# A conformer and Mamba-2 layer on one core: half of the input projection in block products of seven instead of eight

## The chip, the cores and the metric

The kernel runs on one core of one Trainium2 chip. Its time is the device time of one execution in microseconds, and lower is better. Of each kernel the median of several runs is compared; one more execution was profiled. TensorE (PE) does the matrix products, into PSUM; VectorE (DVE) and ScalarE (ACT) do elementwise work and read PSUM; GpSimd (POOL) does next to nothing here; SyncE (SP) issues the DMA transfers.

## The reference, cut to what matters

The layer takes 1024 prompt tokens and 32 sample tokens of 1024 channels. All branches come out of one projection with 11,296 columns:

```
proj = x @ w_in + b_in
a_val, a_glu, a_gate, z, xbc, dt_raw, g_a, g_b, g_p = split(proj)

u = a_val * sigmoid(a_glu)
u = causal_dwconv(u, buf_a, conv_a_w, conv_a_b)                  # width 31
u = silu(layer_norm(u, norm_a_g, norm_a_b)) * silu(a_gate)
out_a = u @ w_a_out

xbc = silu(causal_dwconv(xbc, buf_b, conv_b_w, conv_b_b))         # width 4
xs, B, C = split(xbc)
dt = softplus(dt_raw + dt_bias);  A = -exp(a_log)
y, h_new = ssd_scan(xs, dt, A, B, C, h0)                          # 4 groups of 8 heads, state 128
out_b = gated_rmsnorm(y + d_skip * xs, z, gnorm_w) @ w_b_out

merged = sigmoid(g_a) * out_a + sigmoid(g_b) * out_b
ple = sigmoid(g_p) * (p @ w_ple)
y = layer_norm(alpha * x + merged @ w_out + ple, ln_g, ln_b)
```

Outputs are y, the last rows of both convolutions, and the state of the scan, for prompt and sample. All of it is float32.

## The kernel before

Channels lie on the 128 partitions and tokens on the free axis: 1056 columns, which are the prompt's 1024 and the sample's 32. A large product is a float32 product of three passes. Both operands are split exactly into a rounded part hi and a rest lo (`split`, `w_split`: ACT writes hi, DVE subtracts and writes lo), and `three` (L266) sums hi*lo, lo*hi and hi*hi in PSUM.

The program is a list of slots with equal PE time. A slot (`slot`, L279) multiplies one tile of weights, 1024 x 128, with x: 8 row tiles k, three passes, three column groups of 352, so 72 matmuls. The PSUM banks of the groups rotate over 0, 1, 2. ACT evicts each group, with the bias. The slots run in this order:

- Slot 1, with the 48 matmuls of dt mixed in, as the rows of x arrive (L405 on). dt goes through softplus and sums in the steps `dt1` to `dt10`, laid over the following slots.
- The input projection in 88 slots, by SSM group: a pair of conv-a tiles (glu, val), B, C and four xs tiles of the group, eight gate tiles that are written out to DRAM, another conv-a pair, four z tiles. Two slots of the embedding product p W_ple (`ple`) stand ahead of group 1.
- 16 slots of out_b, 8 of out_a and the merge, and 32 short slots of w_out with the closing LayerNorm, in four quarters of the tokens (268, 268, 264 and 256 columns).

The SSD scan of a group starts two slots behind its last xs tile and runs in nine chunks, one chunk a slot (`ssd_group`): transposes, the product of C and B, the masked decays, the products with the state, and the product S of XS and B that updates the state. S is made in three passes, with XS and B split.

What stands on DVE in a slot is set by hand: `at(slot, stage, function)` puts a step into a stage of a slot, and what is left of the slot is filled from a queue, `run_fill`, up to a limit of estimated DVE time (8000 to 12300 ns). The queue holds the taps of the 31-wide convolution (conv a, L156, 1086 columns each). The 4-wide convolution (conv b) is three taps of 1059 columns for each B, C or xs tile. Weights are loaded two slots ahead and split one slot ahead. All loads and stores go through SP in program order.

SBUF tiles for activations come out of pools of 32 pieces of 1064 columns (T) and five of 1116 (U).

Of the kernel before, what the change touches and what calls it, by code (L numbers as in the profile page):

```python
# [43 lines left out]
WA, WB = NT + LA, NT + LB    # columns that a conv computes  # L44
# [4 lines left out]
G_GATE, G_GA, G_GB = 0, 16, 24        # first gate tile of a kind  # L49


def slot_tiles():
    """(kind, index, first column in w_in) of the slots of the first half."""
    pair = lambda t: [("glu", t, O_GLU + 128 * t), ("val", t, O_VAL + 128 * t)] if t < 8 else []
    out = pair(0)
    for g in range(4):
        if g == 1:
            out += [("ple", 0, None), ("ple", 1, None)]
        out += [("B", g, O_B + 128 * g), ("C", g, O_C + 128 * g)]
        out += [("xs", 4 * g + j, O_X + 128 * (4 * g + j)) for j in range(4)]  # L60
# [29 lines left out]
class Units:  # L90
    """Fixed pieces of SBUF (or PSUM) handed out in program order."""
# [24 lines left out]
def emit(nc, tc, I, O, ctx):  # L116
    cpool = ctx.enter_context(tc.tile_pool(name="const", bufs=1))
    wpool = ctx.enter_context(tc.tile_pool(name="w", bufs=2))
    tpool = ctx.enter_context(tc.tile_pool(name="t", bufs=1))
    dpool = ctx.enter_context(tc.tile_pool(name="scr", bufs=1, space=bass.MemoryType.DRAM))  # L120
    ppool = ctx.enter_context(tc.tile_pool(name="ps", bufs=1, space=bass.MemoryType.PSUM))

    spool = tc.tile_pool(name="ssd", bufs=1)
    sp = spool.__enter__()

    T = Units(tpool, 32, 1064, "t")
    U = Units(tpool, 5, 1116, "u")
# [22 lines left out]
    def tt(out, a, b, op):  # L150
        dve[0] += 75 + 1.04 * width(out)
        nc.vector.tensor_tensor(out, a, b, op)  # L152

    def stt(out, a, s, b, op0, op1):
        dve[0] += 135 + 1.04 * width(out)
        nc.vector.scalar_tensor_tensor(out, a, s, b, op0, op1)  # L156

    def tsc(out, a, s1, s2, op0, op1=None):
        dve[0] += 75 + 0.6 * width(out)
        if op1 is None:  # L160
            nc.vector.tensor_scalar(out, a, s1, None, op0)
        else:
            nc.vector.tensor_scalar(out, a, s1, s2, op0, op1)
# [7 lines left out]
    def mm(out, l, r, start=True, stop=True):  # L171
        nc.tensor.matmul(out, l, r, start=start, stop=stop)  # L172

    # the weights of dt: for each row tile 32 columns of hi, 32 of lo, and 64 that are not looked at
    wdt = T.get([P, 1024], F32R, "wdt")
    wd3 = wdt[:, :].rearrange("p (k c) -> p k c", k=8)
    nc.gpsimd.memset(wd3[:, :, 64:].bitcast(F32), 0.0)

# [38 lines left out]
    todo = defaultdict(list)  # L217
    busy = set()                 # slots that also run SSD products
# [40 lines left out]
    def split(raw, name):  # L259
        hi = tget((P, NT), F32R, name + "h")  # L260
        lo = tget((P, NT), F32R, name + "l")
        act(hi, raw)
        tt(lo, raw, hi[:, :].bitcast(F32), ALU.subtract)
        return hi, lo

    def three(ps, wh, wl, xh, xl, first, last):  # L266
        mm(ps, wh, xl, first, False)
        mm(ps, wl, xh, False, False)
        mm(ps, wh, xh, False, last)
# [9 lines left out]
    def slot(s, nm, nk, rhs, evac):  # L279
        """The products of one slot: nm output tiles with nk operand tiles each."""  # L280
# [39 lines left out]
        run_fill(8000.0 if s < 10 else (11400.0 if s < 25 else 12300.0) if ("pe", s) in busy else 10000.0)  # L320
# [4 lines left out]
    def bcast_pe(src, bks):  # L325
        """Sum over the partitions, on all partitions."""
# [30 lines left out]
        # both parts of V are exact, and so are their products with one  # L357
# [51 lines left out]
    w1raw = wpool.tile([P, 1024], F32, tag="wraw", name="wraw1", bufs=2)
    xraw = []  # L410
    for k in range(8):
        t = tget(name="xraw")
        for c0, c1 in GR if k == 0 else ((0, NT),):
            load(t[:, c0:c1], I["xT"][k * P:(k + 1) * P, c0:c1])
        xraw.append(t)
        if k < 2:
            sl = slice(0, 256) if k == 0 else slice(256, 1024)
            load(w1raw[:, sl], I["w_src"][1][:, sl])
        if k == 3:
            load(par, I["par"])  # L420
# [783 lines left out]
    for x in xT:  # L1204
        tput(*x)
# [213 lines left out]
```

## Time and profile before

| | us |
|---|---|
| median of three runs | 1578.08 |
| lowest and highest of them | 1575.24, 1578.16 |
| span of the profiled execution | 1573.9 |
| PE busy in it | 1559.6 (99%) |
| DVE busy | 1151.5 (73%) |
| ACT busy | 723.6 (46%) |
| mean DMA rate | 128 GB/s |
| mean granted clock of PE | 0.997 |

The profiled execution's own time is its span, from the first to the last instruction. Busy times are the sums of the instructions of an engine, without overlaps; PEld is the loading of weights into the array, which runs beside the products. The ends of matmuls are modelled, so how long one matmul takes in a row of them is read from start to start. The chain that ended last is the sequence of work followed back from the last instruction, each step to what released it. In a line of a timeline the first number is the start, the second the duration.

### The profile page before, as it was taken

Reading aid. Unit: us, or ns where it says so; the run is one execution under the profiler, and the core shown is the slowest. Engines: PE = TensorE matmul, PEld = TensorE weight load, DVE = VectorE, ACT = ScalarE, POOL = GpSimd, SP = SyncE. Lnnn points to the kernel's source line nnn. Section 1 sums busy time; section 2 is a strip of 40 time slices with the busy share of each in tenths; the row PEclk is TensorE's granted clock in tenths of the full one; section 3 lists DMA queues with packets and bytes.
Section 4 is the critical chain, followed back from the end, with each engine's and each line's share of the span. In section 5 each row is a group of like instructions: output and inputs, shape, how many; then the busy total and the mean of one; then the engine's idle time right before and its main releaser. Section 6 shows DMA issues by size and latency. Waiting matters only on the chain.

```text
span 1573.9 us, 25018 instructions
## 1 busy us (share of the span) xinstructions
PE 1559.6 (99%) x10283; PEld 1532.7 (97%) x10283; DVE 1151.5 (73%) x1504; ACT 723.6 (46%) x1257; POOL 3.0 (0%) x14
## 2 busy tenths in 40 slices
PE   8999999999999999999999999999999999999997
PEld 8999999999999999999999999999999999999997
DVE  4769888888448888893988687579877486755554
ACT  5565452354475633346444335554346363423333
POOL 0000000000000000000000000000000000000000
PEclk9999999999999999999999999999999999999999
DMA  5126542234448741144763213466455544323222
GB/s 188 49 61 180 158 135 83 83 121 152 91 96 202 180 147 55 41 137 130 204 200 111 65 52 69 157 193 197 151 206 178 192 141 147 96 96 121 97 84 82
DMA packets 123868, 201.81 MB, mean 128 GB/s; under 512 B 27045, under 2 KB 83109, under 8 KB 123754
## 3 DMA queue, kind: packets, MB, share of 16 engines
q1 hardware_dynamic: 123754, 200.22, 42.6%
q8 instruction: 80, 1.31, 0.4%
q14 instruction: 34, 0.28, 0.1%
HBM read 150.01 MB, written 50.18 MB: 127 GB/s over the span
## 4 chain that ended last, share of the span: by engine, by line
PE 98%; ACT 1%; DVE 1%; issue 0%; DMA 0%; ACTq 0%; SPq 0%; DVEq 0%
PE ps L172 96%; PE ps L703 1%; PE ps L704 0%; DVE dtk_t L544 0%; ACT r_t L166 0%; DVE cb_t L156 0%; ACT dtk_t L166 0%; DMA xraw_t<-in_xT 0%; ACT cbo_t L166 0%; ACT p_t L166 0%; ACT dts_t L166 0%; ACT L166 0%; ACT cb_t L166 0%; ACT vin_t L166 0%; ACT whi L166 0%
## 5 line engine op out<-in xcount | busy, mean ns | idle before, releaser
L152 DVE TENSOR_TENSOR wlo<-wraw,whi 128x1024 fp32r<-128x1024 f32 (+1 forms) x117 | 141.9, 1213 | 162.8 <-ACT whi L166 162.3
L156 DVE SCALAR_TENSOR_TENSOR cae_u<-uin_u,par,cae_u 128x1086 f32<-128x1086 f32 x120 | 161.2, 1344 | 0.0
L166 ACT ACTIVATE whi<-wraw 128x1024 fp32r<-128x1024 f32 (+1 forms) x117 | 122.2, 1045 | 70.7 <-PE ps L172 55.5
L156 DVE SCALAR_TENSOR_TENSOR cao_u<-uin_u,par,cao_u 128x1086 f32<-128x1086 f32 x112 | 150.5, 1344 | 0.0
L156 DVE SCALAR_TENSOR_TENSOR cb_t<-vin_t,par,cb_t 128x1059 f32<-128x1059 f32 x72 | 94.9, 1318 | 17.1 <-ACT cb_t L166 13.6
L166 ACT ACTIVATE vin_t<-ps,par 128x352 f32<-128x352 f32 (+1 forms) x96 | 42.8, 477 | 131.7 <-PE ps L172 131.7
L172 PE MATMUL ps<-x0l_t,whi 128*128 128x352 f32 x264 | 90.1, 341 | 0.2 <-ACT vin_t L166 0.2
L172 PE MATMUL ps<-x0h_t,wlo 128*128 128x352 f32 x264 | 85.9, 325 | 0.0
L172 PE MATMUL ps<-x0h_t,whi 128*128 128x352 f32 x264 | 85.7, 324 | 0.0
L172 PE MATMUL ps<-x2h_t,wlo 128*128 128x352 f32 x264 | 85.4, 323 | 0.0
L172 PE MATMUL ps<-x3h_t,wlo 128*128 128x352 f32 x264 | 85.4, 323 | 0.0
L172 PE MATMUL ps<-x4h_t,wlo 128*128 128x352 f32 x264 | 85.4, 323 | 0.0
L172 PE MATMUL ps<-x3h_t,whi 128*128 128x352 f32 x264 | 85.3, 323 | 0.0
L172 PE MATMUL ps<-x4h_t,whi 128*128 128x352 f32 x264 | 85.3, 323 | 0.0
L172 PE MATMUL ps<-x2h_t,whi 128*128 128x352 f32 x264 | 85.3, 323 | 0.0
L172 PE MATMUL ps<-x1h_t,whi 128*128 128x352 f32 x264 | 85.3, 323 | 0.0
L166 ACT ACTIVATE L_t<-L_t,tk 128x128 f32<-128x128 f32 (+1 forms) x288 | 85.3, 381 | 0.0
L172 PE MATMUL ps<-x2l_t,whi 128*128 128x352 f32 x264 | 85.3, 323 | 0.0
L172 PE MATMUL ps<-x3l_t,whi 128*128 128x352 f32 x264 | 85.3, 323 | 0.0
L172 PE MATMUL ps<-x4l_t,whi 128*128 128x352 f32 x264 | 85.3, 323 | 0.0
L172 PE MATMUL ps<-x5l_t,whi 128*128 128x352 f32 x264 | 85.3, 323 | 0.0
L172 PE MATMUL ps<-x1h_t,wlo 128*128 128x352 f32 x264 | 85.3, 323 | 0.0
(631 smaller groups left out, 4785.2 us busy)
## 6 DMA issues: line engine op xcount, KB each, us to landing
wraw<-in_w SPq DMA_DIRECT2D x87, 512.0 KB, 4.0
L_t<-d_accp SPq DMA_DIRECT2D x32, 512.0 KB, 6.7
d_gate<-gt_t SPq DMA_DIRECT2D x24, 528.0 KB, 5.2
d_yn<-cbo_t SPq DMA_DIRECT2D x16, 528.0 KB, 4.4
yraw_t<-d_yn SPq DMA_DIRECT2D x16, 528.0 KB, 4.7
gs_t<-d_gate SPq DMA_DIRECT2D x16, 528.0 KB, 4.5
cw_t<-in_wo SPq DMA_DIRECT2D x16, 512.0 KB, 5.3
wraw<-in_wb SPq DMA_DIRECT2D x16, 512.0 KB, 3.7
```

What stands on the lines that cost most here:

```text
L152: nc.vector.tensor_tensor(out, a, b, op)
L156: nc.vector.scalar_tensor_tensor(out, a, s, b, op0, op1)
L166: nc.scalar.activation(out, a, f, **kw)
L172: nc.tensor.matmul(out, l, r, start=start, stop=stop)
L703: nc.tensor.transpose(pX[:nt, j * P:(j + 1) * P], XS[j][:, sl], ident)
```

## The change

48 of the 88 projection tiles are taken in 24 pairs. With x cut into two halves of its rows (channels) and two of its columns (tokens), and the two tiles of weights of a pair cut into quarters r11, r12, r21, r22 (the first digit is the tile, the second the half of the rows), the four result blocks are made from seven block products instead of eight. The right operands are fixed for all pairs: B11, D1 = B11 - B12, N2, B21, T3, B22 and T4, with N2 = -(D1 + B22), T3 = B22 - B12 and T4 = -(N2 + B21), formed once at the start (`x_sum`, `x_split`, `t_split`) and kept split. D1 takes the place of B12 in the tiles of x, which is loaded again before the single slots. The left operands are formed for each pair one pair ahead: four sums of quarters and seven splits, 512 columns each (`prep_act`, `prep_dve`).

A block product is 4 row tiles, three passes and two groups of 264 columns: 24 matmuls, 168 a pair. Products 0, 2, 4 and 6 add up in the two banks B0 or B1, by turns, and ACT evicts the running sum after each; products 1 and 5 share the two banks C, and product 3 has A. DVE adds A, product 1 (copied out by ACT) and C to the evicted results.

```
+def pair_tiles():
+    gate = lambda n: ("gate", n, GATE_OFF[n // 8] + 128 * (n % 8))
+    G = lambda n: (gate(n), gate(n + 1))
+    C = lambda t: (("glu", t, O_GLU + 128 * t), ("val", t, O_VAL + 128 * t))
+    X = lambda n: ("xs", n, O_X + 128 * n)
+    return [G(0), G(2), C(0), G(8), G(4), G(10), G(6), C(1), G(12), G(16), G(14), C(2), G(18), G(20), G(22), G(24),
+            C(3), G(26), G(28), G(30), C(4), (("B", 0, O_B), ("C", 0, O_C)), (X(0), X(1)), (X(2), X(3))]
...
+    return ca(5) + bcx(1) + z(0) + ca(6) + bcx(2) + z(1)[:2] + ca(7) + bcx(3) + z(1)[2:] + z(2) + z(3)
...
-    T = Units(tpool, 32, 1064, "t")
-    U = Units(tpool, 5, 1116, "u")
+    T = Units(tpool, 22, 1064, "t")
+    U = Units(tpool, 7, 1116, "u")
...
-        dve[0] += 75 + 1.04 * width(out)
+        dve[0] += 144 + 1.053 * width(out)
...
-        run_fill(8000.0 if s < 10 else (11400.0 if s < 25 else 12300.0) if ("pe", s) in busy else 10000.0)
+        run_fill(14200.0 if ("pe", s) in busy else 11000.0)
...
-                three(S, B2[:nt, :P], B2[:nt, P:], XS2[:nt, :512], XS2[:nt, 512:], True, True)
+                mm(S, B2[:nt, :], M[:nt, :512])
...
+    for m in range(4):
+        for g in range(3):
+            ple_group(m, g)
+            step(2 if m * 3 + g >= 4 else 1)
+    U.put(*praw)
+    step(len(work))
+    for k in range(8):
+        dt_products(k)
+    dt1()
+    pw_hi(0, 0, "r11")
+    pw_lo(0, 0, "r11")
+    x_sum("D1", 0)
+    x_sum("D1", 1)
...
+    def pair_slot(s, oa, ob, ba, bb):
+        for j in range(7):
+            ps = A if j == 3 else C if j in (1, 5) else B
+            wh, wl = pw.pop((i, j))
+            for g in range(2):
+                c = slice(g * HN, g * HN + HN)
+                for k in range(4):
+                    w = slice(k * P, k * P + P)
+                    three(ps[:, g, :HN], wh[:, w], wl[:, w], OPND[j](k, 0)[:, c], OPND[j](k, 1)[:, c],
+                          k == 0 and j in (0, 1, 3), k == 3, j in (2, 4, 5, 6))
...
+            elif j == 6:
+                for p_, d in oa[1]:
+                    tt(d, d, p_(C), ALU.add)
+            prep_act(i, j)
+            prep_dve(i, j)
+            if j == 5:
+                run(s, "d2")
+            run_fill(2820.0 * (j + 1) - 300.0)
...
+    SSD0 = [S_CL + i for i in (1, 10, 21, 31)]
```

Behind the pairs stand 40 single slots as before (conv-a tiles 5 to 7, B, C and xs of groups 1 to 3, all z), and the SSD groups start at the second, 11th, 22nd and 32nd of them. The embedding moves to the very start: its first half, dt, `dt1`, its second half, and only then pair 0. S is one float32 product, with neither operand split. The centring of w_out's columns moves from the projection into out_b and out_a, the variance of branch A's LayerNorm is taken later, in out_b, and pools of pieces are opened as others close.

On PE, a plain slot of before goes from one column group to the next (x5h is the high part of x's row tile 5, whi and wlo the split weights):

```order
L172 MATMUL ps_904<-x7l_t_181,whi_757 128x352
L172 MATMUL ps_904<-x7h_t_180,wlo_759 128x352
L172 MATMUL ps_904<-x7h_t_180,whi_757 128x352
L172 MATMUL ps_930<-x0l_t_135,whi_757 128x352
L172 MATMUL ps_930<-x0h_t_134,wlo_759 128x352
```

In the change, pair 0 goes from product 1 (banks C, here ps_633) to product 2 (banks B, ps_583, into which product 0 went too):

```order
L192 MATMUL ps_633<-x3l_t_111,w_1h 128x264
L192 MATMUL ps_633<-x3h_t_110,w_1l 128x264
L192 MATMUL ps_633<-x3h_t_110,w_1h 128x264
L192 MATMUL ps_583<-n2l_4_517,w_2h 128x264
L192 MATMUL ps_583<-n2h_4_516,w_2l 128x264
```

The matmuls are narrower, the weights change with each product, and product 2 adds to banks that ACT has read in between.

On ACT, the start of before splits w0 (wdt) and then x as it comes:

```order
L166 ACTIVATE wdt_t_74<-w_t_106 128x8x32
L166 ACTIVATE x0h_t_134<-xraw_t_109 128x352 x3
L166 ACTIVATE whi_142<-wraw_108 128x256
L166 ACTIVATE x1h_t_146<-xraw_t_114 128x352 x3
L166 ACTIVATE whi_142<-wraw_108 128x768
```

The change has there, behind the splits of the embedding's operands (pl is the result of the embedding), and later ahead of pair 0's first eviction (ga):

```order
L186 ACTIVATE wq1h<-wq_132 128x512
L186 ACTIVATE pl_u_197<-ps_190 128x352
L186 ACTIVATE wdt<-w_142 128x8x32
L186 ACTIVATE pl_u_197<-ps_201 128x352
L186 ACTIVATE x0h_t_104<-xraw_t_134 128x528
...
L186 ACTIVATE w_4h<-r_0_164 128x512
L186 ACTIVATE t4h_4_568<-xraw_t_134 128x1056
L186 ACTIVATE t4h_4_568<-xraw_t_136 128x1056
L186 ACTIVATE w_5h<-sx_411 128x512
L186 ACTIVATE ga_t_581<-ps_583,par 128x528
```

The split of w0 stands behind an eviction of the embedding, with the splits of x behind it, and the first eviction of pair 0 behind the splits of T4.

On DVE, a B, C or xs tile of before has its conv-b taps between two splits of weights, with nothing of PSUM behind them:

```order
L152 TENSOR_TENSOR wlo_861<-wraw_753,whi_859 128x1024
L163 TENSOR_SCALAR dtk_t_866<-dtk_t_866 128x528
L544 RECIPROCAL dtk_t_866<-dtk_t_866 128x528
L152 TENSOR_TENSOR dtk_t_866<-dtk_t_866 128x528
L152 TENSOR_TENSOR dtk_t_866<-dtk_t_866,dt_t_331 128x264
L156 SCALAR_TENSOR_TENSOR cb_t_876<-vin_t_750,par,cb_t_876 128x1059 x3
L1124 MEMSET vin_t_964 128x3
```

In pair 22 of the change (xs 0 and 1) the taps of the tiles of pair 21 stand ahead of the addition that reads banks C (ps_5893):

```order
L172 TENSOR_TENSOR vin_t_5848<-vin_t_5848 128x232
L172 TENSOR_TENSOR vin_t_5848<-vin_t_5848 128x32
L172 TENSOR_TENSOR w_2l<-sx_5890,w_2h 128x512
L172 TENSOR_TENSOR w_3l<-r_23_5809,w_3h 128x512
L172 TENSOR_TENSOR sx_5890<-r_23_5809,sx_5890 128x512
L176 SCALAR_TENSOR_TENSOR cb_t_5879<-vin_t_5600,par,cb_t_5879 128x1059 x3
L176 SCALAR_TENSOR_TENSOR cb_u_5881<-vin_t_5603,par,cb_u_5881 128x1059 x3
L172 TENSOR_TENSOR vin_t_5845<-vin_t_5845,ps_5893 128x264
L172 TENSOR_TENSOR vin_t_5845<-vin_t_5845,ps_5893 128x232
L172 TENSOR_TENSOR vin_t_5845<-vin_t_5845,ps_5893 128x32
```

Six taps stand between the products' last splits and the addition.

More of the change, by code (lines that the diff above doesn't have):

```diff
@@ L169, in load, with mm @@
         nc.sync.dma_start(dst, src)
[L171 to L177, printed above, removed]
+    def mm(out, l, r, start=True, stop=True, more=False):
+        nc.tensor.matmul(out, l, r, start=start, stop=stop, skip_group_check=more)
     par = cpool.tile([P, NPAR], F32, name="par")
@@ L257, in w_split, with three @@
         wsplit[s] = (hi, lo)
[L259 to L269, printed above, removed]
+    def three(ps, wh, wl, xh, xl, first, last, more=False):
+        mm(ps, wh, xl, first, False, more)
+        mm(ps, wl, xh, False, False, more)
+        mm(ps, wh, xh, False, last, more)
     banks = [0, 1, 2]
@@ L406, in emit @@
     H = 32
-    w0 = tget((P, 8, H), F32, "w0")
-    load(w0, I["wdt"])
[L409 to L420, printed above, removed]
@@ new lines, in emit, with wdt_split @@
+    r_quad(0, 0)
+    r_quad(0, 1)
+    w0 = xpool.tile([P, 8, H], F32, tag="t3l", name="w0", bufs=1)
+    wdt = xpool.tile([P, 1024], F32R, tag="t3h", name="wdt", bufs=1)
+    wd3 = wdt[:, :].rearrange("p (k c) -> p k c", k=8)
+    nc.gpsimd.memset(wd3[:, :, 64:].bitcast(F32), 0.0)
+    load(w0, I["wdt"])
+    r_quad(1, 0)
+    r_quad(1, 1)
+    load(par, I["par"])
+    wq_load(2)
+    wq_load(3)
+    def wdt_split():
+        act(wd3[:, :, :H], w0)
+        tt(wd3[:, :, H:2 * H], w0, wd3[:, :, :H].bitcast(F32), ALU.subtract)
@@ new lines, in ple_group @@
+    def ple_group(m, g):
+        c0, c1 = GR[g]
+        ps = psum(bank())
+        wh, wl = wq[m // 2]
+        for k in range(2):
+            w = slice((m % 2 * 2 + k) * P, (m % 2 * 2 + k) * P + P)
+            three(ps[:, :GN], wh[:, w], wl[:, w], ph[:, k, c0:c1], pl_[:, k, c0:c1], k == 0, k == 1)
+        if g == 0 and m in (4, 6):
+            both = xpool.tile([P, 2, NT], F32, tag=f"t3{'hl'[m // 2 - 2]}", name=f"pl{m}", bufs=1)
+            pls[m], pls[m + 1] = both[:, 0, :], both[:, 1, :]
+        if g == 0 and m < 4:
+            pls[m] = U.get([P, NT], F32, "pl")
+        act(pls[m][:, c0:c1], ps[:, :GN])
+        if g == 2:
+            load(d_ple[m], pls[m])
+            if m < 4:
+                U.put(pls[m])
@@ L587, in emit, with step @@
         at(sl_, stage, fn)
+    work = deque()
+    def step(n):
+        for _ in range(min(n, len(work))):
+            f, *a = work.popleft()
+            f(*a)
+    for n in ("r11", "r21", "r22", "r12"):
+        pw_load(0, n)
+    wq_split(0)
+    for g in range(3):
+        for k in range(2):
+            p_split(k, g)
+    wq_split(1)
+    work.append((wdt_split,))
+    for n in ("B11", "B12", "B21", "B22"):
+        work.extend((x_split, n, k) for k in range(4))
+    work.extend(((wq_split, 2), (wq_split, 3)))
@@ new lines, in emit @@
+    work.extend((x_sum, "N2", q) for q in range(2))
+    work.extend((t_split, "n2", (0, 0), q) for q in range(2))
+    work.extend(((pw_hi, 0, 2, "sx"), (pw_lo, 0, 2, "sx")))
+    work.extend((x_sum, "T3", q) for q in range(2))
+    for m in range(4, 8):
+        for g in range(3):
+            ple_group(m, g)
+            step(1)
+    step(len(work))
+    for n in ("r21", "r22"):
+        pw_load(1, n)
+    pw_hi(0, 3, "r12")
+    pw_lo(0, 3, "r12")
+    for q in range(2):
+        t_split("t3", (0, 1), q)
@@ new lines, in emit, with plain @@
+    x_put((0, 1))
+    x_put((1, 1))
+    pw_sum(0, "sx", "r12", "sx")
+    pw_load(1, "r12")
+    pw_hi(0, 4, "r21")
+    pw_lo(0, 4, "r21")
+    x_sum("T4", 0)
+    x_sum("T4", 1)
+    for q in range(2):
+        t_split("t4", (0, 0), q)
+    x_put((0, 0))
+    x_put((1, 0))
+    pw_hi(0, 5, "sx")
+    new_psum("ps1")
+    def plain(t):
+        return [[(lambda ps, f=lambda u: u: ps[:, :, :HN], t[:, NH * h_:NH * h_ + NH].rearrange("p (g c) -> p g c", g=2))]
+                for h_ in range(2)]
@@ new lines, in emit, with vin_tile, done @@
+    BIAS = lambda i: col(C_BIN + i)
+    def vin_tile(kind, n):
+        vin = tget((P, NT + 2 * LB), F32, "vin")
+        ct = n if kind == "xs" else (16 + n if kind == "B" else 20 + n)
+        nc.vector.memset(vin[:, :LB], 0.0)
+        load(vin[:, LB + TP:2 * LB + TP], I["cache_b"][ct * P:(ct + 1) * P, :])
+        if kind != "xs":
+            BCs[(kind, n)] = []
+        def done(t):
+            if kind == "xs":
+                XSs[n] = t
+            else:
+                BCs[(kind, n)].append(t)
+        return vin, lambda s: conv_b(ct, vin, s, done)
@@ new lines, in half_load, with half_split, b12_load @@
+    def half_load(q):
+        pr["h", q] = raw_tile(("r11", "r21")[q], f"half{q}")
+        load(pr["h", q], I["w_src"][S_CL][:, 512 * q:512 * q + 512])
+    def half_split(q):
+        h_, l_ = split_tile(q, f"half{q}")
+        act(h_, pr["h", q])
+        tt(l_, pr["h", q], h_[:, :].bitcast(F32), ALU.subtract)
+        wsplit.setdefault(S_CL, []).append((h_, l_))
+    def b12_load():
+        raw = xpool.tile([P, 4, NH], F32, tag="n2h", name="b12", bufs=1)
+        for q in range(2):
+            load(raw[:, 2 * q:2 * q + 2, :], I["xT"][2 * q * P:2 * q * P + 2 * P, NH:].rearrange("(k p) c -> p k c", p=P))
+        R[0, 1] = [raw[:, 2 * q:2 * q + 2, :] for q in range(2)]
@@ L1106, in emit, with b12_split @@
+    def b12_split():
+        for k in range(4):
+            x_split("B12", k)
+        R.clear()
+    at(S_CL - 2, "end", half_load, 0)
+    at(S_CL - 2, "end", half_load, 1)
+    at(S_CL - 1, "a1", b12_load)
+    at(S_CL - 1, "d2", b12_split)
+    at(S_CL - 1, "pm", half_split, 0)
+    at(S_CL - 1, "a2", half_split, 1)
+    for i, (ta, tb) in enumerate(PAIRS):
+        s = i + 1
+        cur[0] = s
+        ba, bb = BIAS(2 * i), BIAS(2 * i + 1)
+        (kind, n, _), (kb, nb, _) = ta, tb
         if kind == "glu":
@@ new lines, in emit @@
+        pair_slot(s, oa, ob, ba, bb)
+    guards[0].__exit__(None, None, None)
+    wpool = ctx.enter_context(tc.tile_pool(name="w", bufs=2, reuse_waits="tile"))
+    t2pool = ctx.enter_context(tc.tile_pool(name="t2", bufs=1, reuse_waits="tile"))
+    spool = tc.tile_pool(name="ssd", bufs=1, reuse_waits="tile")
+    sp = spool.__enter__()
+    T.free.extend((t2pool, f"y{i}") for i in range(3))
+    new_psum("ps2")
+    for b in (3, 4, 5, 6, 7, 0, 1, 2):
+        psum(b)
+    banks[:] = [0, 1, 2]
@@ L1197, in emit @@
-        if kind == "ple":
-            slot(s, 4, 2, pT, evac)
-            if n == 1:
-                for x in pT:
-                    tput(*x)
-            continue
-        slot(s, 1, 8, xT, evac)
-    for x in xT:
+                ssd_group(g_, SSD0[g_], Late(4 * g_), BCs[("B", g_)], BCs[("C", g_)])
+        slot(s, 1, 8, X, evac)
+    for x in X:
         tput(*x)
     mg = []
-    banks[:] = [0, 1, 2, 3, 4]
     for s in range(S_OB, S_OA):
+        if s == SSD0[3] + 12:
+            spool.__exit__(None, None, None)
+            x2pool = ctx.enter_context(tc.tile_pool(name="x2", bufs=1, reuse_waits="tile"))
+            T.free.extend((x2pool, f"x{i}") for i in range(2))
+            banks[:] = [0, 1, 2, 3, 4]
```

588 lines of the change are left out of this document (362 added, 226 removed).

## The prediction

> **What bounds the kernel now.** I read the page first: the busy times of the engines and the chain that ended last.
>
> ```profile
> span 1573.9 us, 25018 instructions
> PE 1559.6 (99%) x10283; PEld 1532.7 (97%) x10283; DVE 1151.5 (73%) x1504; ACT 723.6 (46%) x1257; POOL 3.0 (0%) x14
> PE 98%; ACT 1%; DVE 1%; issue 0%; DMA 0%; ACTq 0%; SPq 0%; DVEq 0%
> ```
>
> TensorE (PE) is busy in 99% of the span and carries 98% of the chain. VectorE (DVE) has 422 us free, but over stages that differ. Next, the waits of PE, all there are:
>
> ```profile
> PE ps L172 <- ACT x0h_t L166: 4.3, 1, 4.3
> PE ps L172 <- DVE r_t L152: 2.0, 1, 2.0
> PE ps L172 <- ACT r_t L166: 0.7, 1, 0.7
> PE ps L172 <- ACT vin_t L166: 0.2, 1, 0.2
> ```
>
> Only the 4.3 us to the first product, and 2.7 us near the end, are waits. So time is gained by less matmul work alone, and lost by any wait that the new order brings. Then the windows of a stretch with the SSD scan and of one without it (columns: PE, PEld, DVE, ACT, POOL):
>
> ```profile
> 150.00:240.00 90.00, 90.00 (x634) 86.54 (x633) 75.56 (x118) 41.34 (x91) 0.00 (x0) 1.00 0.54 151
> 253.00:440.00 187.00, 187.00 (x1181) 186.26 (x1181) 138.47 (x142) 81.80 (x132) 0.00 (x0) 1.00 0.39 108
> ```
>
> DVE is busy 84% of the SSD stretch and 74% of the plain one, and PE never stops. Last, the chain, which gives the slots their lengths:
>
> ```profile
> 120.95 11.55 PE ps L172 x72
> ...
> 222.26 0.44 PE ps L703 x4
> 222.70 0.11 PE ps L704
> 222.81 14.57 PE ps L172 x101
> ```
>
> A plain slot is 72 matmuls of 352 columns in 11.55 us, 0.1604 us each. A slot with an SSD chunk is 15.12 us.
>
> **The products.** 48 tiles of the projection leave their 48 slots: 48 x 72 = 3456 matmuls of 352 columns go, 554.4 us at 0.1604. In their place stand 24 x 168 = 4032 of 264 columns. Before has that width in its last stage, w_out, in a stretch where PE had no idle time:
>
> ```profile
> 1525.00 0.28 PE L172 MATMUL ps<-m1l_t,whi 128*128 128x264 f32 x1
> ...
> 1531.93 0.28 PE L172 MATMUL ps<-m4l_t,woh_t 128*128 128x264 f32 x1
> ```
>
> These two stand 57 matmuls apart, so one takes 6.93 / 57 = 0.1216 us: 490.3 us for all, 20.4 us a pair where two slots took 23.1. The term is **-64 us**, from -62 to -66. A matmul's fixed part is small by these rows: 88 columns less are 0.0388 us less, which leaves 0.005 us at no columns.
>
> A rule speaks against this change here. The Trainium skill (TensorE: Matmul & The Clock Gate, section Back-to-back issue gap) gives a sustained spacing of 81 ns at 128 columns and 131 ns at 512, because weight loads count too. An estimate between these two puts 264 columns at 99 ns and 352 at 110, a pair at 16.6 us against 15.9 for two slots, and the term at +17 in place of -64. The rows do not agree: their spacing falls nearly with the columns, so I go by the rows.
>
> **The SSD product S.** The product of XS and B in three passes becomes one float32 product. A chunk of before shows both kinds (the x8 are four float32 products of 128 columns, the x3 are the three passes of 512):
>
> ```profile
> 220.40 1.16 PE L172 MATMUL ps<-cbo_t,hT_t 128*128 128x128 f32 x8
> 221.31 0.95 PE L172 MATMUL ps<-XS,B 128*128 128x512 f32 x3
> 222.10 0.60 PE L703 MATMUL ps<-ident,cbo_t 128*128 128x128 f32 x4
> ```
>
> 512 columns of float32 take 221.31 - 220.40 = 0.91 us, and the three passes 0.79 us from start to start, or 3 x 512 / 352 x 0.1604 = 0.70 by the plain pitch. That is 0.12 to 0.21 us for each of 36 chunks, all on PE: **+6 us**, from +4 to +8. The splits of both operands that go, on ACT and DVE, free those engines in slots where PE never waits for them, and are worth nothing.
>
> **The start.** Before splits x as it lands and computes dt and the first tile with it. After puts half the embedding first, then dt, then the other half, and builds four extra operands (D1, N2, T3, T4) before the third product of pair 0. The bytes that land before w0 are wq0, the embedding input, wq1 and the upper half of x: 0.26 + 1.08 + 0.26 + 2.16 = 3.76 MB. What the queues moved at the start of before:
>
> ```profile
> 0.00:4.00 4.00, 0.00 (x0) 0.00 (x0) 0.42 (x1) 2.02 (x3) 1.94 (x12) 1.00 0.49 141
> 4.00:8.00 4.00, 3.72 (x8) 2.26 (x9) 2.00 (x4) 1.58 (x4) 0.00 (x0) 1.00 0.88 274
> 8.00:12.00 4.00, 4.00 (x17) 3.60 (x17) 2.08 (x4) 2.44 (x6) 0.00 (x0) 1.00 1.03 411
> 12.00:14.00 2.00, 2.00 (x15) 2.00 (x14) 1.60 (x5) 1.93 (x4) 0.00 (x0) 1.00 1.02 417
> ```
>
> The first three windows are 3.30 MB at 12 us; 0.6 MB more (w0 is 0.13) come at 13.4 to 13.7 us. ScalarE (ACT) reaches the split of w0 as its second instruction behind the first embedding splits, and everything behind it waits with it: 16 splits of x of 528 columns, 11 evictions of 352, two weight splits. Their prices, and those of dt, are in ACT's timeline of before:
>
> ```profile
> 12.86 1.09 ACT L166 ACTIVATE x3h_t<-xraw_t 128x1056 fp32r<-128x1056 f32 x1
> ...
> 21.15 1.28 ACT L166 ACT_TABLE_LOAD   x1
> 26.65 1.52 ACT L166 ACTIVATE sg_t<-ps,par 128x352 f32<-128x352 f32 x3 [4.21 <-PE ps L172]
> 28.06 1.05 ACT L166 ACTIVATE whi<-wraw 128x1024 fp32r<-128x1024 f32 x1
> 29.01 0.28 ACT L166 ACTIVATE small<-par 32x1 f32<-32x1 f32 x2
> ...
> 34.08 0.56 ACT L166 ACTIVATE uin_u<-ps,par 128x352 f32<-128x352 f32 x1
> ```
>
> One eviction of 352 is 1.41 / 3 = 0.47 us from start to start; a split of 528 I take as 0.60, a little over half of 1.09. So 0.4 + 16 x 0.60 + 11 x 0.47 + 2 x 0.55 = 16.3 us: ACT is through at 30.0. Then a table load (1.28) and dt1, which took 5.05 us in before (29.01 to 34.06), then the split of the first quarter: DVE can begin the operands at 36.9. Its prices, from its timeline:
>
> ```profile
> 150.70 0.68 DVE L152 TENSOR_TENSOR M<-ps,tk 128x512 f32<-128x512 f32 x1
> 151.30 0.68 DVE L152 TENSOR_TENSOR X<-ps,tk 128x512 f32<-128x512 f32 x1
> ...
> 306.05 1.25 DVE L152 TENSOR_TENSOR cbo_t<-cbo_t,zt_t 128x1056 f32<-128x1056 f32 x1
> 307.21 0.78 DVE L161 TENSOR_SCALAR cao_u<-uin_u,par 128x1086 f32<-128x1086 f32 x1
> ...
> 309.17 1.34 DVE L156 SCALAR_TENSOR_TENSOR cao_u<-uin_u,par,cao_u 128x1086 f32<-128x1086 f32 x1
> 310.43 1.34 DVE L156 SCALAR_TENSOR_TENSOR cae_u<-uin_u,par,cae_u 128x1086 f32<-128x1086 f32 x1
> ```
>
> Start to start, 512 columns are 0.60 us, 1056 are 1.16 and a tap of 1086 is 1.26. From the first quarter's split to the sums of T4, DVE has 9 of 512, 4 of 528 (0.62), 8 of 1056 and 4 with a scalar (1.23): 5.4 + 2.5 + 9.3 + 4.9 = 22.1 us, to 59.0. ACT stands at the split of T4 with the eviction of product 0 behind it; product 2 adds into the same PSUM banks and waits for that eviction. T4's second split (1.0), a quarter's split (0.55) and the eviction (0.62) end at 61.2. By then PE has 228 matmul times of 0.16 to do (144 of the embedding, 48 of dt, 36 worth of 48 narrow ones): 36.6 us. It has lost 24.6 us. Before had done 120 matmuls (19.2 us) when ACT got the first result at 26.6, so it had lost 7.4. PE has nothing from about 53 us, when product 1 is done. What an idle PE costs when it resumes is seen at before's start:
>
> ```profile
> 8.44 0.49 PE L172 MATMUL ps<-x0l_t,whi 128*128 128x352 f32 x1
> 8.73 0.49 PE L172 MATMUL ps<-x0h_t,wlo 128*128 128x352 f32 x1
> ...
> 11.70 0.32 PE L172 MATMUL ps<-x1h_t,wlo 128*128 128x352 f32 x1
> 11.86 0.33 PE L172 MATMUL ps<-x1h_t,whi 128*128 128x352 f32 x1
> ```
>
> The step is 0.29 us, later 0.16; 16 or 17 such slow matmuls are 2.2 us lost. The term is 24.6 + 2.2 - 7.4 = **+19 us**. The low bound is +10 (w0 lands 2 us earlier, dt1 lies half beside other work, no slow matmuls, 2 us of the chain hidden), the high one +25 (instructions cost their durations, 0.08 us more each, and wait for one another).
>
> The Trainium skill (the same page, section What's actually happening) says that the clock of the array is halved after an idle window of about 3.4 us and is back after about as long of work. By it the slow stretch would lose 1.7 us in place of 2.2, and the sum would stand 0.5 lower; the trace of before agrees in the steps of 0.29 us, though not in the granted clock, which its windows above give as 1.00.
>
> **Inside the pairs and behind them.** A pair has on DVE 11 sums and splits of 512 (6.6 us) and three additions out of PSUM (1.9), 8.5 us fixed. The fill lays conv-a taps behind that, about eight (10 us): counted in the order of the instructions, pairs 3 to 21 come to 18.3 to 19.2 us of DVE in 20.4 of PE. That holds, with 1 to 2 us of margin. ACT has seven splits of 512 and four evictions, some 7 us. It breaks in pair 22: six conv-b taps (7.4 us) stand on DVE between the subtraction behind product 4 and the addition that frees banks C, which pair 23 needs 8.8 us after product 4; DVE gets there at about 11.5. That is 3 us. The single slots with SSD chunks have 13.4 us of DVE in 15.1. In out_b the order gives four slots with 14.4, 15.4, 11.9 and 10.7 us in 11.55, because LayerNorm's centring moved there; the last operand of out_a may be 0 to 2 us late. With a late load here and there (0 to 1 us in four pairs) I take **+6 us**, from +1 to +15.
>
> **The sum.** 1573.9 - 64 + 6 + 19 + 6 = 1541 us of span. The median of the runs, 1578.1, stands 4.2 above the profiled span, so the forecast is **1545 us**. The bounds of the terms give 1527 to 1564.
>
> **Rivals.** *The start is free.* If ACT's queue does not hold the splits (w0 early, the embedding's 23 us of products covering the rest), the +19 is gone: 1526. For it: the embedding's products need no x. Against: 3.76 MB stand ahead of w0 and 22 us of DVE behind dt1, both by rows. 0.14.
>
> *DVE sets the pace of the pairs.* At 21.5 us a pair in place of 20.4, 23 x 1.1 = 25 us come on top: 1570. For it: every split waits for its ACT half and three additions wait for PSUM, and the margin is 1 to 2 us. Against: the fill is limited product by product. 0.13, a quarter of it below 1566 and a sixth of it within 0.2% of before.
>
> *DVE's pace beyond break-even, slower.* One mechanism: in a pair, 22 instructions cost their durations, not their starts (+1.8), and stand some 2 us for ACT's halves, so a pair takes 22.5 us: 24 x 2.1 = 50 us, 1595. It is slower than before from 1545 + 33, that is 1.4 us more a pair, 21.8 us. Against: the rows from start to start show the overlap of 0.08 us. 0.07.
>
> *The pitch does not fall with the columns.* At 0.1604 a matmul the pairs cost 647 us, 93 more than before in place of 64 less: 1702. The two rows of 264 columns rule it out, unless products into two banks behave otherwise. The rule of the Trainium skill quoted above points this way (TensorE: Matmul & The Clock Gate, Back-to-back issue gap). 0.01.
>
> *The gain is eaten up.* Several terms at their worse ends together, within 0.2% of before: 0.02.
>
> **How the numbers follow.** The forecast has 0.63. 0.2% is 3.2 us, about what a measurement of this kernel can tell from no change: 1574.9 to 1581.2 is the same. The range takes in the free start and a quarter of the paced pairs, 1523 to 1566; out of it are 0.10 of the paced pairs and 0.10 of the rest. Faster: 0.63 + 0.14 + 0.11 = 0.88; same: 0.02 + 0.02 = 0.04; slower: 0.07 + 0.01 = 0.08.
>
> **What would show it.** Right: 168 matmuls of 264 columns in 20.4 us in the windows of pairs 3 to 21, with no PE wait above 0.5 us; one PE wait of 6 to 9 us near 53 to 61 us, released by ACT's ga; one of about 3 us near pair 23, released by DVE's vin; SSD slots of 15.2 to 15.3 us. Wrong: pairs of over 21 us with waits for DVE's splits (DVE's pace), no wait beyond 3 us before 70 us (the free start), or a pitch of 264 columns above 0.125 us.

## The result, and the profile after

The changed kernel takes **1601.06 us** (median of four runs, 1600.07 to 1601.86), the one before 1577.93 in the same comparison: a ratio of 1.0152, 95% interval 1.0137 to 1.0166. It is slower by 1.5% where 2% faster was forecast. The page of the profile after:

```profile
span 1598.3 us, 26653 instructions
PE 1529.6 (96%) x10823; PEld 1485.9 (93%) x10823; DVE 1295.8 (81%) x1763; ACT 815.5 (51%) x1395; POOL 3.0 (0%) x14
PE 80%; DVE 10%; ACT 4%; issue 2%; DMA 1%; SPq 0%; ACTq 0%; DVEq 0%
```

PE's busy time fell by 30 us, but it no longer carries 98% of the chain: DVE and ACT carry 14%. The waits of PE, the largest five:

```profile
PE ps L192 <- DVE acc_t L172: 20.8, 5, 7.4
PE ps L192 <- ACT ga_t L186: 11.7, 2, 9.9
PE ps L192 <- DVE vin_t L172: 5.3, 1, 5.3
PE ps L192 <- DVE t4l L172: 5.2, 1, 5.2
PE ps L192 <- ACT sg_t L186: 3.8, 1, 3.8
```

The name in a line is what the releaser wrote; the three numbers are the us in total, how often, and the longest. ga_t is the start, and there the forecast holds: product 2 of pair 0 began at 60.73 us, forecast 61.2. t4l is the first product of the program, whose operand bears that name: it began at 5.15 us. vin_t and sg_t are the end of the pairs. The largest, acc_t, are the sums of out_b. One window over out_b, of before and then of after (columns: PE, PEld, DVE, ACT, POOL, granted clock, DMA share, GB/s):

```profile
1187.60:1374.90 187.30, 187.30 (x1167) 187.30 (x1165) 133.96 (x165) 89.30 (x107) 0.00 (x0) 1.00 0.43 147
```

```profile
1172.60:1397.10 224.50, 201.02 (x1199) 196.40 (x1198) 169.86 (x217) 102.71 (x121) 0.00 (x0) 0.95 0.49 175
```

After had reached out_b 15 us sooner than before, and lost 37 there. Its 16 slots are not lengthened evenly. Windows of slots 7, 14 and 15, counted from 0:

```profile
1264.40:1284.10 19.70, 13.57 (x75) 13.28 (x74) 16.70 (x20) 7.81 (x9) 0.00 (x0) 0.86 0.16 54
...
1357.30:1379.20 21.90, 14.54 (x74) 13.99 (x73) 15.56 (x18) 14.95 (x15) 0.00 (x0) 0.77 0.37 125
1379.20:1397.10 17.90, 13.42 (x75) 13.12 (x74) 12.08 (x14) 11.60 (x12) 0.00 (x0) 0.90 0.36 119
```

Three slots of 11.6 us of products took 59.5, which is 24.7 of the 37. In slot 7 DVE has 16.7 us to do (the centring of four LayerNorm tiles and the sums of four more); in slot 14 both DVE and ACT have about 15. What happens in slot 14 stands in ACT's and then DVE's timeline:

```profile
1354.39 1.28 ACT L186 ACT_TABLE_LOAD   x1
1355.68 1.27 ACT L186 ACTIVATE cat_t<-cat_t,par 128x1056 f32<-128x1056 f32 x1
...
1361.13 1.07 ACT L186 ACTIVATE ag_t<-ag_t 128x1056 f32<-128x1056 f32 x1
1362.22 1.28 ACT L186 ACT_TABLE_LOAD   x1
1363.52 2.06 ACT L186 ACTIVATE gs_t<-gs_t 128x1056 f32<-128x1056 f32 x2
```

```profile
1357.92 0.51 DVE L172 TENSOR_TENSOR acc_t<-acc_t,ps 128x352 f32<-128x352 f32 x1
1364.63 1.26 DVE L172 TENSOR_TENSOR acc_t<-acc_t,gs_t 128x1056 f32<-128x1056 f32 x1 [6.20 <-ACT gs_t L186]
1365.81 1.25 DVE L172 TENSOR_TENSOR u0l_t<-cat_t,u0h_t 128x1056 fp32r<-128x1056 f32 x1
1366.98 1.25 DVE L172 TENSOR_TENSOR u1l_t<-cat_t,u1h_t 128x1056 fp32r<-128x1056 f32 x1
1368.15 0.51 DVE L172 TENSOR_TENSOR acc_t<-acc_t,ps 128x352 f32<-128x352 f32 x1
```

ACT works off six silus of branch A and loads a table before it takes the sigmoid of the merge gate. DVE stands 6.20 us for that sigmoid, then does two splits, and only then the addition (1368.15) that frees a PSUM bank. PE, with all banks full, waits.

### The profile page after: what moved, and what is told of

The parts are those of the page before. It is cut to its first block, busy times and chain, and to the rows that moved or that the text cites. A ratio compares the mean times of both kernels' runs of the same rounds, so it can differ in the third digit from the quotient of the medians.

```text
span 1598.3 us, 26653 instructions
## 1 busy us (share of the span) xinstructions
PE 1529.6 (96%) x10823; PEld 1485.9 (93%) x10823; DVE 1295.8 (81%) x1763; ACT 815.5 (51%) x1395; POOL 3.0 (0%) x14
## 4 chain that ended last, share of the span: by engine, by line
PE 80%; DVE 10%; ACT 4%; issue 2%; DMA 1%; SPq 0%; ACTq 0%; DVEq 0%
PE ps L192 78%; DVE cat_t L172 1%; DVE acc_t L172 1%; PE ps L996 1%; ACT L186 1%; DVE yraw_t L176 1%; DVE wlo L172 0%; ACT ag_t L186 0%; DMA d_gate<-ga_t 0%; ACT L_t L186 0%; DVE cb_u L176 0%; DVE cb_t L176 0%; DVE cao_u L176 0%; SPq L189 0%; DVE cae_u L176 0%
## 5 line engine op out<-in xcount | busy, mean ns | idle before, releaser
L172 DVE TENSOR_TENSOR wlo<-wraw,whi 128x1024 fp32r<-128x1024 f32 x65 | 79.3, 1220 | 25.5 <-ACT whi L186 25.1
L186 ACT ACTIVATE whi<-wraw 128x1024 fp32r<-128x1024 f32 x65 | 68.4, 1053 | 22.5 <-PE ps L192 16.5
L192 PE MATMUL ps<-n2l,w_2h 128*128 128x264 f32 x192 | 55.9, 291 | 9.9 <-ACT ga_t L186 9.9
L192 PE MATMUL ps<-t3l,w_4h 128*128 128x264 f32 x192 | 55.5, 289 | 1.7 <-ACT ga_t L186 1.7
L192 PE MATMUL ps<-n2h,w_2h 128*128 128x264 f32 x192 | 55.8, 291 | 0.0
L192 PE MATMUL ps<-n2h,w_2l 128*128 128x264 f32 x192 | 55.4, 288 | 0.0
L192 PE MATMUL ps<-t3h,w_4h 128*128 128x264 f32 x192 | 55.3, 288 | 0.0
L192 PE MATMUL ps<-t3h,w_4l 128*128 128x264 f32 x192 | 55.2, 287 | 0.0
L192 PE MATMUL ps<-t4l,w_6h 128*128 128x264 f32 x192 | 54.8, 285 | 0.0
L192 PE MATMUL ps<-t4h,w_6l 128*128 128x264 f32 x192 | 54.6, 284 | 0.0
L186 ACT ACTIVATE ga_t<-ps,par 128x528 f32<-128x528 f32 x32 | 22.5, 703 | 57.1 <-PE ps L192 57.0
```

What stands on the lines that cost most here:

```text
L186: nc.scalar.activation(out, a, f, **kw)
L192: nc.tensor.matmul(out, l, r, start=start, stop=stop, skip_group_check=more)
```

## The experiments

The theory to test: the time is lost in the order of out_b's work, where bunches on ACT and DVE stand ahead of the additions that free PSUM. The rivals: the amount of DVE work that was moved into out_b (169.86 us against 133.96), and transfers that come late.

**spread** does the same work in another order:

```
-        at(B + 2 + t // 4 * 2, "ld", ca_load, t)
...
-        at(B + 6 + t // 4, "d1", ln_center, t)
...
-        at(B + 12 + t // 3, "a0", u_act, t)
...
+        at(B + t // 4, "ld", ca_load, t)
...
+        at(B + 3 + t // 3, "d1", ln_center, t)
...
+        at(B + 10 + t // 2, "a0", u_act, t)
...
```

> The same work as the change in another order: branch A's LayerNorm is taken two to three slots earlier and three tiles a slot, its scaling and silu two tiles a slot, the sums of w_out's columns and the last quarter's splits in the slots that were light. If the bunches in out_b are the cause (slots 7 and 12 to 15, where DVE and ACT had 16 to 18 us of work in 11.6 of PE), out_b falls from 224.5 us to 190 to 200 and the time by 25 to 34 us, to 1567 to 1576. If the amount of DVE work is the cause (170 us in out_b against 134 before), or the transfers (197 to 256 GB/s there against 147), nothing of it is less here: out_b stays above 216 and the time within 8 us of 1601.

Measured: 1578.31 us, ratio 1.0012 (1.0002 to 1.0021) to before, 23 us less than the change. Out_b as a whole, and slots 14 and 15:

```profile
1174.70:1377.50 202.80, 194.77 (x1199) 190.48 (x1199) 171.88 (x220) 100.27 (x119) 0.00 (x0) 1.00 0.54 195
```

```profile
1353.10:1365.90 12.80, 12.20 (x75) 11.62 (x74) 10.90 (x13) 7.70 (x8) 0.00 (x0) 1.00 0.49 181
1365.90:1377.50 11.60, 11.60 (x74) 11.60 (x74) 10.72 (x15) 5.08 (x5) 0.00 (x0) 1.00 0.68 214
```

DVE's work is no less (171.88 us) and the transfers are faster (195 GB/s), and 22 us are gone. So the order was the cause of that much. The gain is 2 us short of the expected range, and 15 us over before remain in slots 0 to 5.

**no_scale** takes DVE work away without moving anything:

```
+        if k >= 12:
             stt(yraw[k], yraw[k], col(C_GNW + k), rb, ALU.mult, ALU.mult)
```

> Leaves out the scaling of the first 12 operand tiles of out_b by their norms and weights, 12 DVE instructions of 1.24 us, 8 of them in out_b's slots 0 to 7; nothing else is moved. By the bunches only slot 7 gains: 1 to 3 us, 1598 to 1600. By the amount of DVE work, 10 of the 36 us that out_b has more go: about 10 us, 1591. By the transfers nothing: 1601.

Measured: 1588.63 us, 12.4 less. That is nearer to the rival's 10 than to 1 to 3, so the expectation by the bunches was too small. But where the time went is not where the work went. The windows of slots 2 to 5 together and of slot 7:

```profile
1196.40:1246.00 49.60, 49.05 (x302) 48.23 (x300) 32.79 (x40) 21.46 (x32) 0.00 (x0) 1.00 0.57 207
...
1257.90:1272.00 14.10, 11.84 (x74) 11.55 (x72) 13.84 (x16) 3.18 (x4) 0.00 (x0) 1.00 0.22 76
```

In the change slots 2 to 5 take 49.7 us with 36.26 of DVE: four scalings went from them, and nothing was gained. Slots 6 and 7 lost two scalings, 2.6 us of DVE's work, and went from 33.2 to 26.0 us. Slots 0 and 1 gained 2.4 together, and the single slots ahead of out_b 3.0. So less work on DVE helps where a slot is over-full, by more than its own time, and not in the others.

**no_centre** leaves the 24 loads and 16 stores out, and the DVE work with them:

```
...
-        at(S_OB + 5 + i, "d2", cw_sum, i)
...
-        at(S_OA - 1 + i, "d2", cw_center, m)
...
-        at(S_OA - 1 + i, "d2", cb_center, i)
...
```

> Leaves out the centring of w_out and of what is added to its product: 24 loads and 16 stores of half a megabyte, 11 us of DVE in out_b's slots 5 to 12, 2.4 us a slot from slot 15 into out_a. By the bunches a little in slots 7, 12 and 15: 3 to 6 us, 1595 to 1598. By the amount of DVE work 11 to 13 us, 1589. By the transfers, 20 us or more of the 37 that out_b lost, below 1581.

Measured: 1598.90 us, 2.2 less. With 9.5 us of DVE gone from out_b (160.41 in place of 169.86), and 20 MB of transfers from out_b and out_a, neither the transfers nor the amount as such can be the main cause.

**gs_first** moves only the sigmoids on ACT:

```
-        at(s, "a0", g_sig, m)
+        todo[(s, "a0")].insert(m % 2, (g_sig, (m,)))
```

> In out_b's slots 12 to 15 ACT takes the sigmoids of the two merge gates ahead of the silus of branch A instead of behind them; the same work. In slot 14 ACT has 16.0 us of work in 11.6, and DVE stood 11.8 us waiting for these sigmoids. If ACT's queue is what holds the additions there, 8 to 14 of the 17 us that slots 14 and 15 lost come back: 1587 to 1593. If it is DVE's own bunch (16.1 us in slot 14) or the late loads of the gates, less than 4 us: above 1597.

Measured: 1587.84 us, 13.2 less. Slots 14 and 15:

```profile
1357.10:1373.70 16.60, 12.98 (x73) 12.39 (x73) 16.43 (x19) 15.71 (x15) 0.00 (x0) 0.94 0.51 170
1373.70:1385.90 12.20, 12.20 (x73) 12.20 (x73) 12.06 (x15) 8.62 (x9) 0.00 (x0) 0.94 0.50 170
```

39.8 us became 28.8 with the same work. So ACT's queue held 11 of the 16.6 us that these two slots lost; most of the rest is left in slot 14, where DVE and ACT still have 16.4 and 15.7 us of work.

**act_order** tried the same idea in slots 0 to 8, where no_scale had gained:

```
-        at(s, "a0" if k < 12 else "a1", y_hi, k)
-        at(s, "a1" if k < 12 else "a2", y_lo, k)
+        at(s, "a1", y_hi, k)
+        at(s, "a2", y_lo, k)
...
+        if s == S_OB + 1:
+            banks[:] = [0, 1, 2, 3, 4]
```

> The change, with the scaling and splits of out_b's operands placed behind the first eviction of a slot instead of ahead of all, and five PSUM banks in place of three from out_b's second slot on; the same work. Leaving the scaling out gained 12.4 us, all in slots 0 to 8. If that was ACT's queue (evictions behind a split that waits for the scaling, which waits on DVE behind LayerNorm), this order gains 6 to 12 us with the scaling kept: 1589 to 1595. If it was the 10 us of DVE time, it gains less than 3: above 1598.

Measured: 1601.77 us, nothing gained in sum. Out_b is 2.4 us shorter (222.1), 2.2 of them in slots 0 to 2. The single slots ahead of it, where the first splits moved too, are 3 us longer (597.0 against 593.9); they are as long in spread, where these splits stayed, so this is not shown to come from the placing. Slot 7 stays at 19.4. So ACT's evictions behind the splits are a small part of it; what no_scale gained in slots 6 and 7 is DVE's time in slots that are over-full.

**start_t4** moves T4 behind pair 0's first eviction:

```
...
+    def t4_late():
+        x_sum("T4", 0)
+        x_sum("T4", 1)
+        for q in range(2):
+            t_split("t4", (0, 0), q)
...
+    at(1, "ld0", t4_late)
```

> The sums and splits of the operand T4 are emitted behind pair 0's first eviction, so that product 2 no longer waits for them. If ACT's order is what holds product 2, the 9.9 us wait near 50 us falls to 0 to 2 us and the slow matmuls behind it (2.5 us) go: 8 to 12 us less, 1589 to 1593. If DVE is the limit of the start as a whole, the wait comes back within pairs 0 to 2 (for T4's low half or the splits behind it): less than 4 us gained.

Measured: 1601.82 us. The wait for ga_t fell (9.9 to 4.5 us for the longest), and product 2 began at 57.91 us in place of 60.73. The time came back in the first pairs, most of it in waits for splits and additions on DVE, the largest of them for w_5l:

```profile
PE ps L192 <- ACT ga_t L186: 6.8, 2, 4.5
...
PE ps L192 <- DVE w_5l L172: 2.1, 1, 2.1
```

The wait near 173 us, which ended at 175.3 in the change, ends at 176.6 here. DVE, not ACT's order alone, limits the start.

**before_s** puts the one float32 product into the kernel before:

```
-                three(S, B2[:nt, :P], B2[:nt, P:], XS2[:nt, :512], XS2[:nt, 512:], True, True)
+                mm(S, B2[:nt, :], M[:nt, :512])
```

> The kernel before, with S as one float32 product and neither operand split, as the change has it; all else as before. By the prediction's rows a chunk costs 0.12 to 0.21 us more on PE, 36 chunks 4 to 8 us: 1580 to 1584. By the change's chunk slots (15.39 us against 15.12) it is 0.27 each and 10 us: 1586. If the splits that go from ACT and DVE were on the path somewhere, it is nearer to nothing.

Measured: 1583.35 us, 5.3 more than before (ratio 1.0039, 1.0024 to 1.0054). Its chain in the SSD slots:

```profile
178.19 0.44 PE ps L703 x4
178.62 0.11 PE ps L704
178.73 14.72 PE ps L172 x100
```

A slot is 15.27 us against 15.12, 0.15 for each of 36 chunks, inside the two rows' 0.12 to 0.21. The changed kernel has there

```profile
745.97 0.44 PE ps L996 x4
746.41 0.11 PE ps L997
746.52 14.85 PE ps L192 x100
```

15.40 us, so 0.13 a chunk come from elsewhere. From start to start they lie in the 72 matmuls of 352 columns, 11.83 us here and 11.70 in before_s; the product S takes 0.86 us in both. Why the same matmuls are 1% slower in the change stays open.

The end of the pairs took three experiments. **c_first** emits the addition from banks C ahead of the taps, in the last two pairs:

```
...
             if j == 5:
+                if i in (22, 23):
+                    for p_, d in oa[1]:
+                        tt(d, d, p_(C), ALU.add)
                 run(s, "d2")
```

> In the last two pairs the addition that frees banks C is emitted ahead of the conv-b taps instead of behind them. If the taps hold pair 23's second product, the 5.3 us wait near 538 us and its slow matmuls (0.9 us) go: 5 to 7 us less, 1594 to 1596. If DVE is simply behind there, whatever its order, the splits of the next pair come later by as much: less than 2 us gained.

Measured: 1600.92 us, no gain. The wait for vin_t (5.3 us) is gone, the one for sg_t grew from 3.8 us, and one for vin_u came:

```profile
PE ps L192 <- ACT sg_t L186: 6.4, 1, 6.4
...
PE ps L192 <- ACT vin_u L186: 3.0, 1, 3.0
```

**fill_less** gives DVE fewer conv-a taps in the last three pairs:

```
-            run_fill(2820.0 * (j + 1) - 300.0)
+            run_fill(2820.0 * (j + 1) - 300.0 - (7500.0 if i >= 21 and j < 5 else 0.0))
```

> In the last three pairs the queue of conv-a taps gets 7.5 us less until product 5, so that about six taps a pair go to later slots. If DVE is given too much in these pairs (fixed 8.5 us, six conv-b taps 7.4 us, and six or more conv-a taps in 20.4 us), the waits near 538 and 575 us (5.3 and 3.8 us) and their slow matmuls (2.2 us) go: 7 to 11 us less, 1590 to 1594. If the order inside pair 22 alone was the cause, or the taps press on the SSD slots later, it gains less than 3 us.

Measured: 1604.01 us, no gain (ratio to before 1.0170, 1.0145 to 1.0195). In pair 22 DVE now stood idle ahead of the burst of six taps (2.8 and 1.5 us) and behind it (3.3 us), and PE's waits at the end of the pairs were 10.4 us in place of 9.1: amount was not the point. **taps_split** breaks the burst:

```
+            if j == 6:
+                run(s, "d3")
...
+        if s + 2 == S_CL:
+            at(s + 2, "a1", silu)
...
+            fb(s, "d3" if i < 23 else "d2")
```

> In pairs 22 and 23 the conv-b taps of the second tile are emitted behind product 6 and its addition instead of with the first tile's behind product 5, and the silu of the first two xs tiles stands behind the first eviction of the first single slot instead of ahead of it. If the burst of 7.4 us on DVE and the silu waiting for it on ACT are the cause, the waits near 538 and 575 us fall from 9.1 to under 4 us and the slow matmuls go with them: 5 to 9 us less, 1592 to 1596. If DVE's amount in these pairs is the cause, the waits move again, as with c_first: less than 2 us gained.

Measured: 1595.37 us, 5.7 less. The waits near 538 and 575 us are down to 1.3 and 0.4, with one of 2.0 between them:

```profile
PE ps L192 <- ACT vin_u L186: 2.0, 1, 2.0
```

Six taps in one piece, with an addition on one side and splits on the other that PE both needs, were the cause of the first wait; moving the addition alone (c_first) left 9.4 us of waits at the end of the pairs in place of 9.1. The silu that was moved stands behind that wait, but ahead of the one near 575 us, so for the second the run does not tell the two edits apart.

Four combinations. **best1** is spread, act_order and c_first.

> The spread LayerNorm, the placing of act_order and the addition of c_first together. The spread version still has 16 us in out_b over 16 x 11.6, most of it in slots 0 to 5. If the three causes are separate, 23 + 6 + 6 to 10 us go from 1601: 1562 to 1567, faster than both kernels. If DVE's volume in out_b is the floor (its busy time in the spread version is 187 us of 203), the placing gives nothing on top: 1572 or more.

Measured: 1594.65 us, 16 more than spread alone: act_order's placing, behind the first eviction, comes behind LayerNorm's squares there, and slots 3, 4 and 6 grew to 15.8, 19.4 and 17.3 us. **spread_fill** is spread and fill_less.

> The spread LayerNorm and fill_less together. If they are separate causes their gains add: 1578 less 7 to 11 us, 1567 to 1571, faster than before. If the taps that fill_less puts off delay the LayerNorm, which needs all of conv a, it stays at 1576 or above.

Measured: 1577.91 us, as spread. **best2** adds gs_first, the banks, and a part of act_order's placing.

> spread_fill with gs_first, five banks from out_b's second slot on, and the scaling of operand tiles 4 to 6 behind the first eviction (slots 0 to 2 of out_b took 39 us by act_order's placing and 45 in the spread version). Adds up to 1562 to 1567; if the placing takes from slots 3 to 6 what it gives to 0 to 2, as in best1, 1570 or above.

Measured: 1579.22 us: slots 0 to 2 gained 6 us over spread, and slots 3 to 6 lost 9. **best3** is spread, taps_split, gs_first and five banks from slot 1 on.

> The spread version with taps_split, gs_first, and five PSUM banks from out_b's second slot on; operand splits where the change has them. If the three banks are what costs slots 0 to 2 of out_b (45 us in the spread version, 35 at full pace), 4 to 7 us go there, with taps_split's 5 to 9: 1562 to 1569, faster than before. If those slots wait for ACT's queue behind the scaling, only taps_split's share goes: 1570 to 1574.

Measured: 1570.92 us, ratio 0.9962 (0.9950 to 0.9974): faster than both kernels, by 0.4% and 1.9%. With more banks slots 1 and 2 took 25.5 us in place of 29.2, and slot 4 took 17.5 in place of 13.7. The largest wait in out_b:

```profile
PE ps L192 <- DVE y7l_t L172: 3.1, 1, 3.1
```

Out_b takes 201 us there, 14 more than before. Whether that is DVE's amount in slots 0 to 5 (scaling, LayerNorm and the end of the scan together) was not settled.

## Why the prediction was wrong

**The products, -64: nearly right.** The chain shows 120 block products in one piece:

```profile
175.32 354.07 PE ps L192 x2880
```

That is 0.1229 us a matmul, forecast 0.1216: 4032 of them are 495.7 us, and the term is -59. In this stretch PE waited nowhere. The Trainium skill's spacing (TensorE: Matmul & The Clock Gate, Back-to-back issue gap), from which 99 ns were estimated for 264 columns, does not describe these matmuls; the measurement decides. A pair runs at 20.65 us.

**S, +6: right.** 5.3 us by before_s, 0.15 a chunk.

**The start, +19: right, and by the mechanism that was forecast.** Product 2 began at 60.73 (forecast 61.2), and then 26 matmuls came at 0.220 us instead of 0.122, 2.5 us lost (forecast 2.2). With the same 36.6 us of work done and 7.4 lost in before, the term is 24.1 + 2.5 - 7.4 = +19. DVE worked on the operands without a pause from 35.96 us (forecast 36.9) to the end of T4's sums at 58.45 (forecast 59.0):

```profile
35.96 0.69 DVE L172 TENSOR_TENSOR w_0l<-r,w_0h 128x512 fp32r<-128x512 f32 x1 [1.78 <-ACT w_0h L186]
...
56.03 2.42 DVE L176 SCALAR_TENSOR_TENSOR xraw_t<-xraw_t,xraw_t 128x1056 f32<-128x1056 f32 x2
```

ACT's order, the eviction behind the splits of T4, was only the last link: with T4 out of the way DVE kept PE waiting.

**The stalls, +6 with bounds +1 to +15: this is the step that failed.** Out_b alone is +37, of which a better order won back 22; the other 15 were not explained. The forecast counted DVE's time in four slots of out_b, got 14.4 and 15.4 us in two of them, and made of that "0 to 2 us late" for out_a's last operand. Three things were missing. None of the four loads comes near the 16.7 us that DVE had in slot 7. ACT's time was not counted, and ACT held slots 14 and 15 (gs_first: 11 us there, 13 in all). And it was not asked what stands behind the late instruction on DVE: not one operand of a later stage, but the additions that empty PSUM for the running one. Where DVE falls behind in this stage, PE stops within a slot. The end of the pairs was counted as 3 us and cost 9.1 of waits and 3.6 of slow matmuls (20 of 0.220 us and 12 of 0.29), since the taps stand in front of two waits and not one.

**The rivals.** The slower rival had a chance of 0.07, and its number (1595) is near the result by chance, for its mechanism did not occur: the pairs ran at 20.65 us, not 22.5, with DVE at 91% of the stretch:

```profile
176.00:563.00 387.00, 381.73 (x3092) 381.35 (x3091) 352.41 (x444) 156.70 (x265) 0.00 (x0) 0.99 0.34 111
```

I looked for the bound where the new work was put, and it appeared where old work had been moved to make room. The range's upper end rested on +15 for the stalls, a bound with no row under it for a stage whose order had been rewritten.

**The sum.** Over the forecast are: products +5, stalls in out_b +36, at the end of the pairs +10, SSD slots +4, and two waits of 2 us near 173 and 1150 us +3, which are 5 with the slow matmuls behind the second (those behind the first lie in the products) less the 2 that the forecast held for late loads. That is 58 us by this count, where 57 lie between 1541 and 1598. The stages behind out_b are 2 us longer (201.2 against 199.0) and are not in it, so the count is good to a few us and not to one.

## What to carry to other kernels

When a change frees time in one stage by moving work to another, the second stage has to be costed slot by slot and engine by engine, as carefully as the first. For each slot that is over-full, ask what is queued behind the late instruction; if it is an instruction that empties PSUM for the running products, the whole excess lands on TensorE, and an in-order wait on another engine (a sigmoid behind six silus) counts as load too. A burst of 7 us on an engine with two customers was mended here by splitting it, not by moving it past one of them.

## What the runs showed of the hardware that was not expected

PE's steps can become slow after a short idle. In the trace of the change PE was idle 1.74 us near 173.6 us:

```profile
173.30 0.29 PE L192 MATMUL ps<-x7h_t,w_3h 128*128 128x264 f32 x1
175.32 0.39 PE L192 MATMUL ps<-t3l,w_4h 128*128 128x264 f32 x1 [1.74 <-ACT ga_t L186]
175.55 0.29 PE L192 MATMUL ps<-t3h,w_4l 128*128 128x264 f32 x1
...
176.23 0.42 PE L192 MATMUL ps<-t3l,w_4h 128*128 128x264 f32 x1
176.45 0.42 PE L192 MATMUL ps<-t3h,w_4l 128*128 128x264 f32 x1
```

The windows behind this idle show the granted clock at 0.50 and then at 1.00:

```profile
176.10:179.50 3.40, 3.40 (x17) 3.40 (x17) 3.37 (x6) 0.40 (x1) 0.00 (x0) 0.50 0.21 75
179.50:183.00 3.50, 3.50 (x31) 3.50 (x30) 3.50 (x4) 2.26 (x4) 0.00 (x0) 1.00 0.42 152
```

A few steps of 0.12 to 0.23 us, and then 0.220 from 176.23 to 179.31 us: about 3 us of slow steps, 1.5 us lost, from an idle of half that length. The Trainium skill (TensorE: Matmul & The Clock Gate, What's actually happening) gives an idle window of about 3.4 us as what halves the clock, and the slow stretch is near its 3.4 us; the idle that set it off here was shorter. The prediction had read slow steps beside a granted clock of 1.00 at the start of before; here the clock shows them.

Not every idle of this length does it. At the same place spread's PE was idle 1.93 us, up to 175.87 us, and its clock stayed at 1.00:

```profile
175.90:179.30 3.40, 3.40 (x28) 3.40 (x29) 3.40 (x6) 0.84 (x2) 0.00 (x0) 1.00 0.03 7
```

In the change the idles of 1.0 to 1.6 us (at 36.5, 38.9, 1180.0, 1262.4, 1355.3 and 1402.2 us) left it at 1.00 as well. So a wait can cost more than its own length, and the long ones did: in slots 14 and 15 of out_b the granted clock was 0.77 and 0.90, and of the 16.6 us that they lost some 4.7 are PE's slower steps (PE busy 14.54 and 13.42 us where 11.6 were due), the rest is idle.
